# Float16 split of attention probabilities: the high part on ScalarE, with one copy of the row scale

## The chip, the core and the metric

The kernel runs on one core of one Trainium2 chip. The metric is the device time of one execution in microseconds; the kernel before has a median of 892.89 us over 3 runs (891.52 to 894.52).

Five engines share the work, each with its own instruction queue that it works off in order: TensorE (PE; its weight loads are listed as PEld), VectorE (DVE), ScalarE (ACT), GpSimd (POOL), and SyncE (SP), which issues all the DMAs. An engine that meets an instruction whose input is not ready waits, and all that stands behind it waits too.

## The reference

One layer of a streaming encoder on 1024 frames of width 1024. A layer norm, one wide input projection, two attentions side by side (8 heads each), a gated output projection of each, their sum through a last projection, and a post layer norm with residual:

```python
h = layer_norm(x, ln_in_g, ln_in_b)
proj = h @ w_in[l] + b_in[l]
a_q, a_k, a_v, a_z, b_cq, b_ckv, b_kr, b_z, g_a, g_b = jnp.split(proj, pts, axis=-1)
...
s = jnp.einsum('bqhd,bkhd->bhqk', qc, kc) * scale + bias      # mixer A, own chunk and 8 before
p = jax.nn.softmax(s, axis=-1)
ya = jnp.einsum('bhqk,bkhd->bqhd', p, vc)
...
s = jnp.einsum('bqhd,bkhd->bhqk', qb, k) * scale              # mixer B, chunk-causal
p = jax.nn.softmax(s, axis=-1)
yb = jnp.einsum('bhqk,bkhd->bqhd', p, v)
...
mixed = jax.nn.sigmoid(g_a) * ya + jax.nn.sigmoid(g_b) * yb
h = layer_norm(DEEPNORM_ALPHA * h + mixed @ w_out[l], ln_post_g[l], ln_post_b[l])
```

The two softmaxes, and in them the multiplication of the exponentials by the inverse of their row sum, are what the change is about.

## The kernel before, in words

To keep float32 accuracy, every operand of a matmul is split into a high part and a low part. For the dense projections (class `Chunk`, helper `three`, lines 167 to 169) that makes three matmuls: high by high, high by low, low by high. For P.V, the probabilities `p` are scaled by 2^14 and split into two float16 numbers, `hi` = float16(p) and `lo` = float16(p - hi); V is split likewise into the two halves of a 128-column block.

The attention is cut into steps: one head `e` of a head pair `p`, one tile `i` of 128 query rows. Mixer A has 64 steps (stage A, 175 to 390 us) with 128 to 640 key columns each, mixer B 64 steps (stage B, 400 to 740 us) with 128 to 1024. A step is function `softmax` (line 805) and, some steps later, function `pv` (line 822):

- `pair.scores`: TensorE forms the scores in PSUM (lines 692, 693 for A; 789 to 791 for B). VectorE brings them to SBUF with scale and bias and forms the row minimum `nm` (line 697 for A, 796 for B).
- line 808: ScalarE takes the exponential in place, and the row sum `su`.
- line 810: VectorE forms the reciprocal `rc`; line 812: VectorE forms `rc2` = rc * 2^14.
- line 816: GpSimd forms `hi`, with `rc` as a column scale and 2^14 as a constant.
- line 817: VectorE forms `lo` from the exponentials, `rc2` and `hi`.
- line 819: SyncE issues one DMA that transposes `hi` and `lo` into `pT`.
- line 831: TensorE multiplies `pT` with V into `y`; after every fourth step ScalarE (line 721), VectorE (722) and GpSimd (728) finish the head's half.

A step's `pv` is issued 3 steps later in A (`LAG_A`) and 2 steps later in B (`LAG_B`). Between the steps lies dense work for TensorE: projections of coming heads and of the gates, handed out in units by function `run`. Their results leave PSUM through ScalarE and VectorE (lines 642 and 643 for q and k of A, 639 and 640 for B, 710 to 713 for the z gates, 288 for the output gates). Their weights are loaded by SyncE (line 135), copied as high part by ScalarE (131) and subtracted by GpSimd (132). In the last head pair of A and in B the values of B are scaled by GpSimd (531), cast by ScalarE (533) and subtracted by GpSimd (534).

The kernel is written for a tile framework. Python issues the operations in the order above, but the framework's scheduler decides in which order they stand in each engine's queue, from its own estimates. So a change of one operation moves others.

Of the kernel before, what the change touches and what calls it, by code (L numbers as in the profile page):

```python
# [10 lines left out]
F32 = mybir.dt.float32  # L11
F32R = mybir.dt.float32r
I32 = mybir.dt.int32
AF = mybir.ActivationFunctionType
ALU = mybir.AluOpType
# [3 lines left out]
P = 128  # L19
# [36 lines left out]
def tile_hybrid_layer(  # L56
# [25 lines left out]
    V, A, G, SY = nc.vector, nc.scalar, nc.gpsimd, nc.sync  # L82
# [11 lines left out]
    sm = ctx.enter_context(tc.tile_pool(name="sm", bufs=6))  # L94
# [532 lines left out]
    with ExitStack() as p1:  # L627
# [177 lines left out]
        def softmax(pair, e, i, nm_):  # L805
            s, nm, n = pair.scores(e, i)
            su = sm.tile([P, 1], F32, tag="su", name=f"su{nm_}")
            A.activation(s[:, :n], s[:, :n], AF.Exp, scale=-1.0, bias=nm, accum_out=su)  # L808
            rc = sm.tile([P, 1], F32, tag="rc", name=f"rcp{nm_}")
            V.reciprocal(rc, su)  # L810
            rc2 = sm.tile([P, 1], F32, tag="rc2", name=f"rcs{nm_}")
            V.tensor_scalar(rc2, rc, 2.0 ** 14, None, op0=ALU.mult)
            W_ = pools["w"]
            p16 = pools["p"].tile([P, 2 * W_], F16, tag="p16", name=f"p16{nm_}")
            hi, lo = p16[:, :n], p16[:, n : 2 * n]
            G.tensor_scalar(hi, s[:, :n], rc, 2.0 ** 14, op0=ALU.mult, op1=ALU.mult)  # L816
            V.scalar_tensor_tensor(lo, s[:, :n], rc2, hi, op0=ALU.mult, op1=ALU.subtract)  # L817
            pT = pools["pt"].tile([P, 2 * W_ // P, P], F16, tag="pt", name=f"pT{nm_}")
            SY.dma_start(pT[:, : 2 * n // P, :], p16[:, : 2 * n], transpose=True)
            return pT  # L820
# [18 lines left out]
        class Steps:  # L839
# [7 lines left out]
            def one(self):  # L847
                pair, e, i = self.seq[self.at]
                self.at += 1
                nm = f"{self.m}_{2 * pair.p + e}_{i}"  # L850
                self.q.append((pair, e, i, softmax(pair, e, i, nm)))
                if i == 6:
                    self.next_head()
                if len(self.q) > self.lag:
                    self.fin()
# [111 lines left out]
        with ExitStack() as pb:  # L967
# [7 lines left out]
            for p in range(4):  # L975
                u = sb.units(16)
                if p < 3:
                    n = pairsB[p + 1]
# [110 lines left out]
    for j in range(NT):  # L1089
        n = 4 if j == last else 2  # L1090
# [68 lines left out]
```

## Time and profile before

| what | value |
|---|---|
| median of 3 runs | 892.89 us (891.52 to 894.52) |
| the profiled execution | 892.41 us |
| its span, first to last instruction | 890.6 us |
| mean granted clock of TensorE | 0.977 |
| busy: PE, DVE, POOL, ACT | 832.0, 570.3, 397.3, 359.0 us |
| the low part (line 817), stages A and B | 58.2 and 70.2 us |
| the high part (line 816), stages A and B | 45.6 and 49.7 us |

The busy time of an engine is the time in which it has an instruction under way. TensorE's instructions overlap, so its busy share says little of how fast it works; what it waits for, and the granted clock, say more. In a list of waits, "A <- B" reads: A's engine sat idle before A until B was done.

### The profile page before, as it was taken

How to read it: one execution, taken by the hardware profiler on the slowest of the kernel's cores; microseconds unless marked ns; L12 is line 12 of the kernel's file. 1: busy time of each engine (PE TensorE's matmuls, PEld its weight loads, DVE VectorE, ACT ScalarE, POOL GpSimd, SP SyncE). 2: the span in 40 equal slices, each digit the busy share in tenths (PEclk: the TensorE clock that was granted, in tenths of full speed). 3: DMA queues.
4: the chain of work that ended last, by engine and by line, in shares of the span. 5: the costliest groups of instructions: out<-in, count | busy, mean ns of one | idle time of the engine just before them, and what ended most of it. 6: DMA issues, size and time to landing. Idle time of an engine off the chain costs nothing. (4 is left out here: it accounts for less than half of the span.)

```text
span 890.6 us, 13773 instructions
## 1 busy us (share of the span) xinstructions
PE 832.0 (93%) x4760; PEld 697.9 (78%) x4760; DVE 570.3 (64%) x1267; ACT 359.0 (40%) x729; POOL 397.3 (45%) x413
## 2 busy tenths in 40 slices
PE   5999899998999896999999999999998899999996
PEld 4999798887777685778787877888777787888886
DVE  6899655577687769756655655265606584657654
ACT  4234475445455535545443444354425251422000
POOL 5547541344554445834333943253445373641100
PEclk8999899999999999899999999999999899999999
DMA  6522013376678564595665567556866879551421
GB/s 204 204 106 80 32 42 101 139 150 134 147 150 173 128 145 115 99 206 115 141 154 148 107 153 149 163 119 133 186 176 134 197 194 288 178 165 60 142 95 47
DMA packets 185365, 124.68 MB, mean 140 GB/s; under 512 B 146160, under 2 KB 149744, under 8 KB 185296
## 3 DMA queue, kind: packets, MB, share of 16 engines
q1 hardware_dynamic: 185296, 123.82, 56.0%
q8 instruction: 37, 0.61, 0.3%
q14 instruction: 32, 0.26, 0.1%
HBM read 57.98 MB, written 22.81 MB: 91 GB/s over the span
## 5 line engine op out<-in xcount | busy, mean ns | idle before, releaser
L167 PE MATMUL dn<-hT,wh_c 128*128 128x512 f32 x512 | 206.6, 404 | 5.4 <-DVE sK L643 2.3
L169 PE MATMUL dn<-hT,wl_c 128*128 128x512 f32 x512 | 203.8, 398 | 0.0
L168 PE MATMUL dn<-hT,wh_c 128*128 128x512 f32 x512 | 203.3, 397 | 0.0
L132 POOL TENSOR_TENSOR wl_c<-wr_c,wh_c 128x512 fp32r<-128x512 f32 x64 | 86.1, 1346 | 117.7 <-ACT wh_c L131 103.2
L167 PEld LDWEIGHTS dn<-hT,wh_c 128*128 128x128 f32 x512 | 97.8, 191 | 24.6 <-DVE bQ L640 2.4
L169 PEld LDWEIGHTS dn<-hT,wl_c 128*128 128x128 f32 x512 | 97.6, 191 | 20.1
L168 PEld LDWEIGHTS dn<-hT,wh_c 128*128 128x128 f32 x512 | 97.9, 191 | 18.1
L817 DVE SCALAR_TENSOR_TENSOR p<-sbs,rcs,p 128x128 f16<-128x128 f32 (+3 forms) x64 | 70.2, 1099 | 24.7 <-POOL p L816 22.9
L816 POOL TENSOR_SCALAR p<-sbs,rcp 128x128 f16<-128x128 f32 (+3 forms) x64 | 49.7, 777 | 75.0 <-DVE rcp L810 57.8
L131 ACT ACTIVATE wh_c<-wr_c 128x512 fp32r<-128x512 f32 x64 | 40.3, 630 | 84.0 <-DMA wr_c<-in_wch_dram 61.2
L817 DVE SCALAR_TENSOR_TENSOR p<-ss,rcs,p 128x640 f16<-128x640 f32 (+2 forms) x64 | 59.2, 936 | 21.0 <-POOL p L816 19.9
L808 ACT ACTIVATE sbs<-sbs,nmb 128x128 f32<-128x128 f32 (+3 forms) x64 | 49.5, 774 | 56.1 <-DVE sbs L796 49.1
L728 POOL TENSOR_TENSOR yt<-yt,sz 64x512 f32<-64x512 f32 x32 | 43.4, 1355 | 52.5 <-DVE yt L722 35.7
L816 POOL TENSOR_SCALAR p<-ss,rcp 128x640 f16<-128x640 f32 (+2 forms) x64 | 45.6, 717 | 41.5 <-DVE rcp L810 27.9
L808 ACT ACTIVATE ss<-ss,nm 128x640 f32<-128x640 f32 (+2 forms) x64 | 44.4, 694 | 46.4 <-DVE nm L697 39.3
L831 PE MATMUL y<-pT,v16b 128*128 128x128 f16 x576 | 45.4, 222 | 8.6 <-DMA pT<-p 8.4
L169 PE MATMUL ops<-wo,mixT 128*128 128x512 f32 (+1 forms) x144 | 53.1, 369 | 0.0
L168 PE MATMUL ops<-wo,mixT 128*128 128x512 f32 (+1 forms) x144 | 52.9, 369 | 0.0
L831 PEld LDWEIGHTS <-v16b 128*128 128x128 f16 x576 | 33.5, 99 | 23.8 <-issue 22.6
L831 PE MATMUL y<-pT,v16a 128*128 128x128 f16 x480 | 38.4, 223 | 14.6 <-DMA pT<-p 13.4
L167 PE MATMUL ops<-wo,mixT 128*128 128x512 f32 (+1 forms) x144 | 51.7, 369 | 0.0
L831 PEld LDWEIGHTS <-v16a 128*128 128x128 f16 x480 | 28.8, 99 | 26.2 <-issue 21.1
(247 smaller groups left out, 1891.2 us busy)
## 6 DMA issues: line engine op xcount, KB each, us to landing
wr_c<-in_wch_dram SPq DMA_DIRECT2D x64, 256.0 KB, 3.1
th_d<-g SPq DMA_DIRECT2D x32, 256.0 KB, 2.5
th<-th_d SPq DMA_DIRECT2D x32, 256.0 KB, 3.3
h_d<-xt SPq DMA_DIRECT2D x8, 512.0 KB, 2.6
sX<-sQ SPq DMA_DIRECT2D x16, 256.0 KB, 4.6
sXb<-bQ SPq DMA_DIRECT2D x16, 256.0 KB, 3.9
r<-h_d SPq DMA_DIRECT2D x8, 512.0 KB, 3.5
wor<-in_wo_dram SPq DMA_DIRECT2D x16, 256.0 KB, 2.9
```

The costliest lines, as they stand in the source:

```text
L131: A.activation(hi, raw, AF.Copy)
L132: (eng or V).tensor_tensor(lo, raw, f(hi), op=ALU.subtract)
L167: T.matmul(ps, ah, bh, start=start, stop=False)
L168: T.matmul(ps, ah, bl, start=False, stop=False)
L169: T.matmul(ps, al, bh, start=False, stop=stop)
L728: G.tensor_tensor(yt[r, :], yt[r, :], pair.sz[half][r, :], op=ALU.mult)
L808: A.activation(s[:, :n], s[:, :n], AF.Exp, scale=-1.0, bias=nm, accum_out=su)
L816: G.tensor_scalar(hi, s[:, :n], rc, 2.0 ** 14, op0=ALU.mult, op1=ALU.mult)
L817: V.scalar_tensor_tensor(lo, s[:, :n], rc2, hi, op0=ALU.mult, op1=ALU.subtract)
L831: T.matmul(o, v16[:, k0 + k, h % 4, :], pT[:, a * nk + k, :], start=(k == 0 and a == 0), stop=(k == nk - 1 and a == 1))
```

## The change

ScalarE forms `hi`, with a copy activation whose column scale is `rc2`; GpSimd no longer has a part in the softmax. The separate tile `rc` goes: VectorE first multiplies the row sum by 2^-14 and then takes the reciprocal in place, which gives rc * 2^14 as before. Since a line fewer stands in the file, lines behind 810 shift by one: the high part is line 815 now, the low part 816, the transposing DMA 818, P.V 830.

```diff
             A.activation(s[:, :n], s[:, :n], AF.Exp, scale=-1.0, bias=nm, accum_out=su)
-            rc = sm.tile([P, 1], F32, tag="rc", name=f"rcp{nm_}")
-            V.reciprocal(rc, su)
             rc2 = sm.tile([P, 1], F32, tag="rc2", name=f"rcs{nm_}")
-            V.tensor_scalar(rc2, rc, 2.0 ** 14, None, op0=ALU.mult)
+            V.tensor_scalar(rc2, su, 2.0 ** -14, None, op0=ALU.mult)
+            V.reciprocal(rc2, rc2)
             W_ = pools["w"]
             p16 = pools["p"].tile([P, 2 * W_], F16, tag="p16", name=f"p16{nm_}")
             hi, lo = p16[:, :n], p16[:, n : 2 * n]
-            G.tensor_scalar(hi, s[:, :n], rc, 2.0 ** 14, op0=ALU.mult, op1=ALU.mult)
+            A.activation(hi, s[:, :n], AF.Copy, scale=rc2)
             V.scalar_tensor_tensor(lo, s[:, :n], rc2, hi, op0=ALU.mult, op1=ALU.subtract)
```

The scheduler places the 128 high parts among ScalarE's other instructions, and moves others on all engines. First place: ScalarE's queue in the third head of A (head 2), steps 3 to 7. The names: `ss` the exponentials, `su` the row sums, `p` high and low part, `rcs` the row scale, `yl` the half of P.V that ScalarE takes out of PSUM, `zt` and `sz` the z gate, `wh_c` the high part of a weight. Before:

```order
L808 ACTIVATE ss_4_2736,su_2_4_2739<-ss_4_2736,nm_4_2737 128x640
L131 ACTIVATE wh_c_1_2616<-wr_c_1_2615 128x512
L808 ACTIVATE ss_5_2766,su_2_5_2769<-ss_5_2766,nm_5_2767 128x640
L808 ACTIVATE ss_6_2803,su_2_6_2806<-ss_6_2803,nm_6_2804 128x640
L131 ACTIVATE wh_c_0_2851<-wr_c_0_2850 128x512
L721 ACTIVATE yl_2_0_2833<-y_2_0_2717,us_101 64x512
L808 ACTIVATE ss_7_2874,su_2_7_2877<-ss_7_2874,nm_7_2875 128x640
```

and now:

```order
L808 ACTIVATE ss_4_2716,su_2_4_2719<-ss_4_2716,nm_4_2717 128x640
L131 ACTIVATE wh_c_1_2599<-wr_c_1_2598 128x512
L808 ACTIVATE ss_5_2745,su_2_5_2748<-ss_5_2745,nm_5_2746 128x640
L815 ACTIVATE p_2_4_2724<-ss_4_2716,rcs_2_4_2721 128x640
L815 ACTIVATE p_2_5_2753<-ss_5_2745,rcs_2_5_2750 128x640
L131 ACTIVATE wh_c_0_2828<-wr_c_0_2827 128x512
L808 ACTIVATE ss_6_2781,su_2_6_2784<-ss_6_2781,nm_6_2782 128x640
L721 ACTIVATE yl_2_0_2810<-y_2_0_2697,us_101 64x512
L815 ACTIVATE p_2_6_2789<-ss_6_2781,rcs_2_6_2786 128x640
```

The high part of step 4 now stands behind a weight copy and the exponential of step 5, and the exponential of step 6 stands behind two high parts and a weight copy.

Second place: the change from head 6 to head 7 of A (347 to 374 us in the trace). `vs_b` and `v16b` are the values of B, `bK` keys of B. GpSimd's queue before:

```order
L728 TENSOR_TENSOR yt_5_1_4094<-yt_5_1_4094,sz_1_3530 64x512
L531 TENSOR_TENSOR vs_b_0_4099<-v16b_3394,vsc_b_4044 128x256
L816 TENSOR_SCALAR p_6_5_4201<-ss_5_4192,rcp_6_5_4197 128x640
L531 TENSOR_TENSOR vs_b_1_4129<-v16b_3394,vsc_b_4044 128x256
L531 TENSOR_TENSOR vs_b_2_4162<-v16b_3394,vsc_b_4044 128x256
L816 TENSOR_SCALAR p_6_6_4230<-ss_6_4221,rcp_6_6_4226 128x640
L534 TENSOR_TENSOR v16b_3394<-vs_b_0_4099,v16b_3394 128x4x64
L816 TENSOR_SCALAR p_6_7_4296<-ss_7_4287,rcp_6_7_4292 128x640
```

ScalarE's queue there now:

```order
L808 ACTIVATE ss_7_4232,su_6_7_4235<-ss_7_4232,nm_7_4233 128x640
L710 ACTIVATE zt_0_4129<-dn_0_3947,bcolh 128x512
L712 ACTIVATE sz_0_4131<-dn_0_3947,bcol 128x512
L808 ACTIVATE ss_0_4269,su_7_0_4272<-ss_0_4269,nm_0_4270 128x128
L533 ACTIVATE v16b_3358<-vs_b_1_4077 128x4x64
L639 ACTIVATE bK_4113<-bk_0_4115 64x512
L533 ACTIVATE v16b_3358<-vs_b_2_4109 128x4x64
L808 ACTIVATE ss_1_4323,su_7_1_4326<-ss_1_4323,nm_1_4324 128x256
L815 ACTIVATE p_6_7_4240<-ss_7_4232,rcs_6_7_4237 128x640
```

On GpSimd the high parts stood between the scalings of the values of B; on ScalarE the high part of head 6, step 7 stands behind seven other instructions that come after its exponential.

## Rows read from the trace of the kernel before

**Rows 1.** Page, part 1: busy us, share of the span, instructions.

```profile
PE 832.0 (93%) x4760; PEld 697.9 (78%) x4760; DVE 570.3 (64%) x1267; ACT 359.0 (40%) x729; POOL 397.3 (45%) x413
```

**Rows 2.** Windows, stages A, B: length; PE, PEld, DVE, ACT, POOL busy; clock, DMA.

```profile
175.00:390.00 215.00, 195.05 (x1216) 160.25 (x1215) 160.49 (x387) 110.37 (x230) 114.10 (x136) 0.97 0.67 140
400.00:740.00 340.00, 325.70 (x1858) 266.40 (x1857) 193.09 (x460) 145.85 (x285) 156.64 (x149) 0.98 0.67 152
```

**Rows 3.** Waits of PE, stage A, then B: us in total, times, longest.

```profile
PE y L831 <- DMA pT<-p: 13.4, 13, 2.0
PE y L831 <- DMA pT<-p: 8.4, 6, 2.6
```

**Rows 4.** Timeline, DVE and POOL, A's first and last step: start, us.

```profile
174.78 0.16 DVE L810 RECIPROCAL rcp<-su 128x1 f32<-128x1 f32 x1 [0.22 <-ACT ss L808]
174.98 0.15 DVE L812 TENSOR_SCALAR rcs<-rcp 128x1 f32<-128x1 f32 x1
175.12 0.38 POOL L816 TENSOR_SCALAR p<-ss,rcp 128x128 f16<-128x128 f32 x1
...
386.46 0.15 DVE L810 RECIPROCAL rcp<-su 128x1 f32<-128x1 f32 x1
386.97 1.57 POOL L816 TENSOR_SCALAR p<-ss,rcp 128x640 f16<-128x640 f32 x2
```

**Rows 5.** Groups by form: busy us, mean ns of one | idle before.

```profile
L816 POOL TENSOR_SCALAR p<-ss,rcp 128x640 f16<-128x640 f32 x32 | 28.4, 891 | 16.8 <-DVE rcp L810 13.9 <-issue 2.7
L808 ACT ACTIVATE ss<-ss,nm 128x640 f32<-128x640 f32 x32 | 26.5, 827 | 21.3 <-DVE nm L697 19.3 <-DVE rcs L812 1.2 <-DVE rcp L810 0.6
L401 ACT ACTIVATE ct<-ct,rr 128x256 f32<-128x256 f32 x8 | 4.1, 509 | 3.7 <-POOL rr L128 3.5
L808 ACT ACTIVATE ss<-ss,nm 128x256 f32<-128x256 f32 x8 | 4.0, 501 | 1.3 <-POOL p L816 1.3
L817 DVE SCALAR_TENSOR_TENSOR p<-ss,rcs,p 128x640 f16<-128x640 f32 x32 | 36.0, 1138 | 6.6 <-POOL p L816 5.9 <-DVE rcp L810 0.3
L697 DVE CUSTOM_DVE_ANT_0 ss<-sa,tb 128x640 f32<-128x640 f32 x32 | 26.0, 817 | 2.0 <-PE sa L693 1.7
```

**Rows 6.** Page, part 5: the exponentials of stages B and A.

```profile
L808 ACT ACTIVATE sbs<-sbs,nmb 128x128 f32<-128x128 f32 (+3 forms) x64 | 49.5, 774 | 56.1 <-DVE sbs L796 49.1
L808 ACT ACTIVATE ss<-ss,nm 128x640 f32<-128x640 f32 (+2 forms) x64 | 44.4, 694 | 46.4 <-DVE nm L697 39.3
```

**Rows 7.** Windows of line 816 alone, stages A and B: length, POOL busy.

```profile
175.00:390.00 215.00, 45.63 (x64) 0.97 0.67 140
400.00:740.00 340.00, 49.70 (x64) 0.98 0.67 152
```

**Rows 8.** Timeline of ACT, in the second place shown.

```profile
354.97 0.59 ACT L639 ACTIVATE bK<-bk 64x512 fp32r<-64x512 f32 x1
...
356.52 0.69 ACT L710 ACTIVATE zt<-dn,bcolh 128x512 f32<-128x512 f32 x1 [0.21 <-DMA y_d<-yt]
```

**Rows 9.** Waits of ACT and DVE, stage A.

```profile
ACT ss L808 <- DVE nm L697: 35.7, 23, 3.9
ACT wh_c L131 <- DMA wr_c<-in_wch_dram: 16.9, 9, 3.7
DVE p L817 <- POOL p L816: 19.9, 26, 2.6
```

**Rows 10.** Timeline of POOL and DVE near 365 us.

```profile
365.29 0.67 POOL L534 TENSOR_TENSOR v16b<-vs_b,v16b 128x256 f16<-128x256 f32 x1
365.35 1.47 DVE L817 SCALAR_TENSOR_TENSOR p<-ss,rcs,p 128x256 f16<-128x256 f32 x1 [2.64 <-POOL p L816]
```

**Rows 11.** Timeline of PE: two matmuls of 512 columns.

```profile
179.69 0.39 PE L167 MATMUL dn<-hT,wh_c 128*128 128x512 f32 x1
179.92 0.39 PE L168 MATMUL dn<-hT,wh_c 128*128 128x512 f32 x1
```

**Rows 12.** Windows, head 6 to head 7 of A.

```profile
347.00:374.00 27.00, 21.38 (x126) 16.88 (x125) 21.47 (x51) 17.81 (x41) 23.06 (x26) 0.87 0.59 106
```

## The prediction

> **What bounds the kernel now.** I read the page's busy times first. TensorE (PE) is busy 832.0 us, 93% of the span; VectorE (DVE), GpSimd (POOL) and ScalarE (ACT) stand at 64, 45 and 40% [rows 1]. So the question for the change is not how much work it moves but whether TensorE waits more or less. The change touches only the attention, so I cut the trace into its two stages, A (175 to 390 us) and B (400 to 740 us) [rows 2]. There TensorE is idle 215 - 195.05 = 20.0 us and 340 - 325.70 = 14.3 us, and its mean granted clock is 0.97 and 0.98, which costs another 215 x 0.03 + 340 x 0.02 = 13.3 us, or 0.39 us for each us of idle time. VectorE fills 75% of stage A, ScalarE 51%, GpSimd 53%; in B 57, 43 and 46%.
>
> The waits tell which work comes late. TensorE's largest are for the transposed probabilities: 13.4 us in 13 waits in A and 8.4 us in 6 in B [rows 3], 21.8 us together. They are the only stake that the change can reach directly. A softmax step runs: score matmuls, scaling and row minimum (VectorE), exponential with row sum (ScalarE), reciprocal (VectorE), high part (GpSimd), low part (VectorE), transposing DMA, P.V matmuls. TensorE works in program order, so what counts is the margin between the landing of a transposed tile and the moment at which TensorE gets to it.
>
> **The change, part by part.** There are 128 steps, 64 in each stage.
>
> 1. The high part leaves GpSimd. In the timeline I paired each reciprocal with the high part that follows it: the first pair waits 0.18 us, and the last (the second of the two merged high parts, which starts near 387.74) 1.13 us [rows 4]. Over 64 pairs each the mean is 0.78 us in A and 0.47 us in B. That is GpSimd's queue, and it goes.
>
> 2. The operation itself. GpSimd takes 891 ns for 640 columns. ScalarE's price for a float16 output with a column scale from SBUF has no row; the nearest are the exponential at 640 columns, 827 ns, and, for the form, the copy with a column scale at 256 columns, 509 ns beside 501 ns for the exponential [rows 5]. So I price it as the exponential: over all forms it gains 0.03 us a step in A and 0.01 in B. The bounds are -0.1 and +0.1 us.
>
> 3. VectorE's two small operations keep their number. Before, GpSimd needed only the reciprocal; now ScalarE needs both, so one more of 0.15 us with its hand-over stands in the chain [rows 4]: +0.19 us a step.
>
> 4. ScalarE's load. 64 high parts at the exponential's price are 44.4 us in A and 49.5 us in B [rows 6]. ScalarE goes to 154.8 of 215 us (72%) in A and to 195.4 of 340 us (57%) in B. GpSimd falls by its 45.6 and 49.7 us [rows 7].
>
> 5. ScalarE's queue, the disputed term. In the new order, counted over the whole program, 2.1 other ScalarE instructions stand between a step's exponential and its high part in A, 1.2 in B; by the durations of their forms 1.41 and 0.81 us. VectorE needs some 0.95 us (A) and 0.70 us (B) in that time anyway for its two small operations. Only what exceeds this delays the high part: taken step by step, 0.68 us in A and 0.33 us in B. The second place shown is an extreme: seven instructions between, about 4.0 us by their forms, among them a gate evacuation at 0.69 and a key half at 0.59 us [rows 8].
>
> 6. Waits inside that queue. ScalarE too works in order, and those instructions wait themselves: in A exponentials wait 35.7 us for VectorE's minimum, 0.56 us each over 64, and weight copies 16.9 us for their load, 0.77 us each over 22 [rows 9]. An exponential stands between in 30 of 64 steps, a weight copy in 18: 0.56 x 30/64 + 0.77 x 18/64 = 0.48 us a step at most. None of it counts where VectorE's small operations are late for the same reason. Between 0 and 0.48 I take 0.25 us, in both stages.
>
> 7. The low part on VectorE. It takes 1138 ns at 640 columns, where the 640-column operation with only one SBUF tensor takes 817 [rows 5]; it stretches when GpSimd works beside it, as at 365.35 us (1.47 us for 256 columns, beside a GpSimd subtraction) [rows 10]. Of 46 low parts that were slowed by more than 0.1 us, 35 overlapped a two-input GpSimd operation, which stays. So the relief is between 0 and 0.25 us a step; I take 0.05, and leave it out of the sum. The Trainium skill ("GPSIMD Engine Reference", Specifications) says that GpSimd's SBUF interface is shared with VectorE and contends with VectorE instructions that have two SBUF inputs. The trace agrees as far as the stretched low parts go; by that rule alone the relief would be the larger one, which is a rival below.
>
> 8. Cover on TensorE. The scheduler has reordered its matmuls too. Pricing each 512-column matmul by the 0.23 us from start to start [rows 11] and the other forms likewise, 10.75 us of matmuls stood between a step's last score matmul and its first P.V matmul in A, and 11.17 us stand there now: +0.42 us. In B it is 13.32 and 13.23: -0.08.
>
> **The sum.** Chain in A: 0.19 + 0.68 + 0.25 - 0.78 - 0.03 = +0.31 us against +0.42 of cover; in B 0.19 + 0.33 + 0.25 - 0.47 - 0.01 = +0.29 against -0.08. On the mean that is nearly level, but waits are one-sided: a step that gains where nobody waited gives nothing. So I took each of the 128 steps' margins in the trace (minus the wait where TensorE waited), added its own change of cover and subtracted its own change of chain. The negative margins sum to 27.4 us before and 33.7 us after: +6.3. The rows put down 21.8 of those 27.4 us as waits, so I take 0.8 of it, 5.0 us. More idle time lowers the clock; 0.39 of it would be 2.0 us, and I take half, since the grant falls only in some stretches: the costliest, 347 to 374 us, has 0.87 and GpSimd busy 23.06 of 27 us [rows 12]. Together +6.0 us. The profiled execution took 892.41 us, 0.48 below the median of the three runs: 898.4 us.
>
> **The rivals.**
>
> *GpSimd's backlog was the trouble: faster.* At 347 to 374 us GpSimd is the fullest engine beside TensorE, and the high parts stand in one queue with its casts and subtractions. If ScalarE is free whenever VectorE delivers the scale, terms 5 and 6 vanish, and the same count over the steps gives 18.5 us: -8.9 x 0.8 = -7.1, with half the clock's share -1.4, so 883.9 us. It decides at a mean queue wait on ScalarE of about 0.68 us in A: below that the kernel gains. For it speak ScalarE's short operations, 0.4 to 0.8 us; against it the new order, which puts the high part behind others in 60 of 64 steps of A.
>
> *Level.* If the waits inside the queue never count, the count is 27.2 us: 892.3 us. For it speaks the added cover.
>
> *The port.* If removing the high parts takes the whole stretch off the low parts (0.22 us a step in A, 0.28 in B, 32 us of VectorE's time), that cancels term 6: again near 892.3 us. Against it stand the 35 of 46. The skill's rule named above would have it so.
>
> *Head of the line.* If the whole 0.48 us counts, the count is about 42.4 us: +15.0 x 0.8 = 12.0, and 2.3 of clock: 906.7 us. For it speaks that a weight load stands on the DMA queue behind transposes that wait for the low part, so that a late high part makes the next weight copy late.
>
> *The change doesn't do what it says.* The order excludes it: all 128 rows left GpSimd and stand on ScalarE, and no further table load appears.
>
> **How the numbers follow.** About 0.3%, 2.7 us, is what a measurement of this kernel can tell from no change. My forecast, 898.4 us, has 0.33, the head of the line 0.12: slower 0.45. Level has 0.17 and the port 0.08: same 0.25. The backlog has 0.30: faster. The range must hold most of the backlog case and of the head of the line: 881 to 912 us. The likeliest case's own range is 895 to 904.
>
> **What would show it.** The exponential-priced high part: 0.75 to 0.90 us at 640 columns on ScalarE. ScalarE busy near 155 us in A. TensorE's waits for transposed tiles: above 25 us if I am right, below 16 if the backlog was the trouble. The low part at 640 columns: above 1.05 us if GpSimd's two-input operations stretch it, near 0.88 if the port rival holds. VectorE's waits for the high part (19.9 us in A before [rows 9]) should grow. I am wrong if TensorE waits less although ScalarE's queue holds the high part longer than 0.7 us: then the cover, not the chain, decides.

## The result and the profile after

The changed kernel took **881.55 us** (median of 4 runs, 880.07 to 882.12) where the kernel before, on the same chip, took 892.83 us (4 runs, 891.52 to 894.52): a ratio of **0.987, with a 95% interval of 0.9849 to 0.9891**. I had forecast 898.4 us. The sign was wrong; the time lies at the low end of the range (881 to 912 us). A second measurement beside other kernels gave 882.18 us and 0.9867 [0.9837, 0.9897].

First the busy times of the page, the line that answers to [rows 1], and then the windows of stages A and B, which answer to [rows 2] (length; PE, PEld, DVE, ACT, POOL busy; clock, DMA):

```profile
PE 827.7 (94%) x4760; PEld 693.2 (79%) x4760; DVE 554.0 (63%) x1267; ACT 441.9 (50%) x857; POOL 299.6 (34%) x285
```

```profile
175.00:390.00 215.00, 198.04 (x1249) 161.82 (x1248) 156.07 (x392) 149.35 (x296) 69.55 (x77) 0.98 0.73 145
400.00:740.00 340.00, 332.02 (x1906) 271.91 (x1905) 180.60 (x456) 188.66 (x341) 108.64 (x87) 0.99 0.70 161
```

The move itself stands there much as forecast: ScalarE took on 83 us (forecast 93.9), GpSimd lost 98 us (forecast 95.3). What was not forecast is in the DVE column. VectorE has the same 1267 instructions, and yet 16.3 us less work over the span (570.3 to 554.0), 4.4 us less in the window of A and 12.5 in that of B. The page's groups of instructions show where. Of the kernel before, the low parts of stages B and A, and then of the changed kernel (busy us, mean ns of one | idle before):

```profile
L817 DVE SCALAR_TENSOR_TENSOR p<-sbs,rcs,p 128x128 f16<-128x128 f32 (+3 forms) x64 | 70.2, 1099 | 24.7 <-POOL p L816 22.9
L817 DVE SCALAR_TENSOR_TENSOR p<-ss,rcs,p 128x640 f16<-128x640 f32 (+2 forms) x64 | 59.2, 936 | 21.0 <-POOL p L816 19.9
```

```profile
L816 DVE SCALAR_TENSOR_TENSOR p<-sbs,rcs,p 128x128 f16<-128x128 f32 (+3 forms) x64 | 57.1, 898 | 28.3 <-ACT p L815 27.8
L816 DVE SCALAR_TENSOR_TENSOR p<-ss,rcs,p 128x640 f16<-128x640 f32 (+2 forms) x64 | 54.6, 867 | 19.8 <-ACT p L815 18.9
```

The same 128 low parts cost 129.4 us before and 111.7 us now: 13.1 us less in B, 4.6 us in A. All of VectorE's saving is this one line.

The waits of TensorE in stages A and B, to hold against [rows 3]:

```profile
PE y L830 <- DMA pT<-p: 10.2, 16, 1.7
PE y L830 <- DMA pT<-p: 3.9, 5, 1.7
```

They fell from 21.8 to 14.1 us. The high part on ScalarE, its exponential and the low part at 640 columns in stage A, by form, to hold against [rows 5]:

```profile
L808 ACT ACTIVATE ss<-ss,nm 128x640 f32<-128x640 f32 x32 | 26.4, 826 | 13.9 <-DVE nm L697 9.0 <-DVE rcs L810 2.5 <-DVE rcs L811 2.1
L815 ACT ACTIVATE p<-ss,rcs 128x640 f16<-128x640 f32 x32 | 25.8, 821 | 2.8 <-ACT ss L808 1.4 <-DMA pT<-p 1.4
...
L816 DVE SCALAR_TENSOR_TENSOR p<-ss,rcs,p 128x640 f16<-128x640 f32 x32 | 32.9, 1036 | 10.9 <-ACT p L815 10.4
```

And the waits of ScalarE and VectorE in stage A, to hold against [rows 9]:

```profile
ACT ss L808 <- DVE nm L697: 22.6, 22, 3.7
ACT wh_c L131 <- DMA wr_c<-in_wch_dram: 13.7, 8, 3.2
```

```profile
DVE p L816 <- ACT p L815: 18.9, 21, 3.8
```

I took the chain of every step apart (start of the exponential to landing of the transposed tile; means over 64 steps). In **stage A it got longer**, 8.20 to 8.66 us: the wait in the queue of the engine that forms the high part rose from 0.78 us (GpSimd) to 1.04 us (ScalarE), and the time from the low part's end to the landing, which no term of the prediction has, from 3.85 to 4.06 us. In **stage B it got shorter**, 8.06 to 7.77 us: that wait stayed (0.47 to 0.46), the low part fell from 1.10 to 0.90 us, and the gap ahead of it from 0.37 to 0.21. So in A TensorE waits less behind a longer chain, which the prediction had named as the sign that it was wrong.

Why the low part got shorter is seen in one step of stage B. Timeline of GpSimd and VectorE in the kernel before (start, us):

```profile
446.37 0.80 POOL L816 TENSOR_SCALAR p<-sbs,rcp 128x640 f16<-128x640 f32 x1 [1.84 <-DVE rcs L812]
447.13 1.29 POOL L132 TENSOR_TENSOR wl_c<-wr_c,wh_c 128x512 fp32r<-128x512 f32 x1
447.20 1.91 DVE L817 SCALAR_TENSOR_TENSOR p<-sbs,rcs,p 128x640 f16<-128x640 f32 x1 [0.18 <-POOL p L816]
```

and of the same step in the changed kernel:

```profile
441.05 1.29 POOL L132 TENSOR_TENSOR wl_c<-wr_c,wh_c 128x512 fp32r<-128x512 f32 x1 [4.77 <-ACT wh_c L131]
...
442.36 0.83 ACT L815 ACTIVATE p<-sbs,rcs 128x640 f16<-128x640 f32 x1 [0.62 <-DVE rcs L811]
...
443.21 0.69 ACT L288 ACTIVATE g<-dn,bcolh 128x512 f32<-128x512 f32 x1
443.22 0.88 DVE L816 SCALAR_TENSOR_TENSOR p<-sbs,rcs,p 128x640 f16<-128x640 f32 x1 [0.95 <-ACT p L815]
```

Before, the end of the high part released two things at the same moment: VectorE's low part, and GpSimd's own queue, whose next entry, a weight subtraction, had waited behind it. The two ran side by side, and the low part took 1.91 us, where the same step's low part takes 0.88 in the changed kernel. Now a weight subtraction stands 2 us ahead of the low part, beside other work of VectorE; what starts together with the low part is a ScalarE operation, and nothing stretches. Against the shortest durations in the kernel before at each width (0.35 us at 128 columns to 1.28 at 1024), 42 of the 128 low parts were longer by over 0.3 us before, 19 are now: 20 to 15 in A, but 22 to 4 in B. Every one of them overlapped a GpSimd instruction. And 54 low parts started within 0.2 us of a GpSimd instruction's start before, 16 do now.

### The profile page after: what moved, and what is told of

Its sections match the earlier page's. It is cut to its first block, busy times and chain, and to the rows that moved or that the text cites. A ratio compares the mean times of both kernels' runs of the same rounds, so it can differ in the third digit from the quotient of the medians.

```text
span 879.3 us, 13755 instructions
## 1 busy us (share of the span) xinstructions
PE 827.7 (94%) x4760; PEld 693.2 (79%) x4760; DVE 554.0 (63%) x1267; ACT 441.9 (50%) x857; POOL 299.6 (34%) x285
## 5 line engine op out<-in xcount | busy, mean ns | idle before, releaser
L167 PE MATMUL dn<-hT,wh_c 128*128 128x512 f32 x512 | 204.7, 400 | 2.1 <-DVE bQ L640 1.0
L169 PE MATMUL dn<-hT,wl_c 128*128 128x512 f32 x512 | 201.3, 393 | 0.0
L168 PE MATMUL dn<-hT,wh_c 128*128 128x512 f32 x512 | 200.8, 392 | 0.0
L132 POOL TENSOR_TENSOR wl_c<-wr_c,wh_c 128x512 fp32r<-128x512 f32 x64 | 83.9, 1310 | 226.8 <-ACT wh_c L131 214.5
L167 PEld LDWEIGHTS dn<-hT,wh_c 128*128 128x128 f32 x512 | 96.7, 189 | 20.2 <-DVE bQ L640 1.4
L168 PEld LDWEIGHTS dn<-hT,wh_c 128*128 128x128 f32 x512 | 96.7, 189 | 17.5
L816 DVE SCALAR_TENSOR_TENSOR p<-sbs,rcs,p 128x128 f16<-128x128 f32 (+3 forms) x64 | 57.1, 898 | 28.3 <-ACT p L815 27.8
L816 DVE SCALAR_TENSOR_TENSOR p<-ss,rcs,p 128x640 f16<-128x640 f32 (+2 forms) x64 | 54.6, 867 | 19.8 <-ACT p L815 18.9
L810 DVE TENSOR_SCALAR rcs<-su 128x1 f32<-128x1 f32 x128 | 19.3, 152 | 62.4 <-ACT sbs L808 45.2
L815 ACT ACTIVATE p<-sbs,rcs 128x128 f16<-128x128 f32 (+3 forms) x64 | 48.8, 771 | 13.0 <-ACT sbs L808 7.2
L796 DVE TENSOR_SCALAR_CACHE_REDUCE sbs<-sb 128x128 f32<-128x128 f32 (+3 forms) x64 | 47.9, 755 | 1.5
L830 PE MATMUL y<-pT,v16a 128*128 128x128 f16 x480 | 39.0, 223 | 10.2 <-DMA pT<-p 10.2
```

Source lines behind the costliest of these rows:

```text
L132: (eng or V).tensor_tensor(lo, raw, f(hi), op=ALU.subtract)
L167: T.matmul(ps, ah, bh, start=start, stop=False)
L168: T.matmul(ps, ah, bl, start=False, stop=False)
L169: T.matmul(ps, al, bh, start=False, stop=stop)
L796: V.tensor_scalar(s[:, :n].rearrange("p (b w) -> p b w", b=nb), ps[:, :nb, :w], -B_SCALE, None, op0=ALU.mult, op1=ALU.min, accum_out=nm,)
L810: V.tensor_scalar(rc2, su, 2.0 ** -14, None, op0=ALU.mult)
```

## The experiments

Two theories stood at the start. **Place**: what counts is that GpSimd stands no longer between the row scale and the low part. **Load**: what counts is that GpSimd does less, through VectorE's stretched operations. A third soon came in, the **order**: the scheduler had also laid out TensorE's matmuls anew. To part these I held TensorE's matmuls to a given order with ordering edges that add no semaphore wait; the scheduler still ordered the other engines. Ratios are against runs of the kernel before on the same chip.

**1. TensorE's order alone, and the engine alone.** The changed kernel with TensorE's matmuls in the order of the kernel before, and the kernel before with those of the changed one:

```
+ at = [k for a, n in TENSOR_ORDER for k in range(a, a + n)]
+ for a, b in zip(at, at[1:]):
+     tc.add_manual_dep(mm[b], mm[a].name, info, reason="tensor order")
```

> The change as it is (high part on ScalarE), but with TensorE's 4760 matmuls held to the order in which they stood before the change. Order theory (the scheduler's new TensorE order gives the late probabilities more cover): the gain goes, 889 to 893 us. Port theory (the low part on VectorE is no longer stretched by GpSimd) and backlog theory (GpSimd's queue held the high part up): the gain stays, 880 to 885 us.

Measured: 886.25 us, 0.9926 [0.9901, 0.9951].

> The kernel before (high part on GpSimd), but with TensorE's matmuls held to the order that the change got. Order theory: 881 to 886 us. Port and backlog theories: no gain, 890 to 895 us.

Measured: 897.05 us, 1.0043 [1.0024, 1.0061]. The change pays in the old order; the new order under GpSimd's chain is a loss. The order theory fell in its simple form: the order is no gift of its own. But the change in the old order gives only 0.74% of the 1.3%, so the rest needs the order that was laid out for it.

**2. The change in one stage only.** In each kernel the other stage keeps the old lines:

```
+ if isinstance(pair, PairA):
+     V.tensor_scalar(rc2, su, 2.0 ** -14, None, op0=ALU.mult)
+     V.reciprocal(rc2, rc2)
+ else:
+     rc = sm.tile([P, 1], F32, tag="rc", name=f"rcp{nm_}")
+     V.reciprocal(rc, su)
+     V.tensor_scalar(rc2, rc, 2.0 ** 14, None, op0=ALU.mult)
...
+ if isinstance(pair, PairA):
+     A.activation(hi, s[:, :n], AF.Copy, scale=rc2)
+ else:
+     G.tensor_scalar(hi, s[:, :n], rc, 2.0 ** 14, op0=ALU.mult, op1=ALU.mult)
```

The second kernel has `PairB` in place of `PairA`.

> The change in the 64 steps of mixer A alone; mixer B keeps GpSimd. Port theory: of the 17 us by which the low parts got shorter 13 lie in B, so A alone brings little, 888 to 892 us. Order theory: A has the added cover (+0.42 us a step against -0.08 in B), so A alone brings most of it, 881 to 886 us. Backlog theory: most in A as well, since GpSimd's queue held the high part up for 0.78 us there and for 0.47 us in B.

Measured: 887.42 us, 0.9942 [0.9917, 0.9966].

> The change in the 64 steps of mixer B alone; mixer A keeps GpSimd. Port theory: most of the gain, 882 to 886 us. Order and backlog theories: little, 888 to 893 us.

Measured: 891.49 us, 0.9977 [0.9954, 0.9999]. Both stages gain, and A, where the chain became longer, not less than B. The two intervals together reach the 1.3%, their middles give 0.8%, so whether the stages add up is not settled by this. It speaks against a reckoning by the low parts alone: 13 of the 17 us by which they got shorter lie in B, for which B alone was expected at 882 to 886 us.

**3. GpSimd's load put back, first in a form that misled.** An unused copy on GpSimd beside each ScalarE high part:

```
+ junk = pools["j"].tile([P, W_], F16, tag="junk", name=f"jk{nm_}")
+ G.tensor_scalar(junk[:, :n], s[:, :n], rc2, None, op0=ALU.mult)
  A.activation(hi, s[:, :n], AF.Copy, scale=rc2)
```

> The changed kernel, with TensorE's matmuls held in its own order, and beside each ScalarE high part a copy of the same operation on GpSimd (same input, same scale, same width, result never used). GpSimd's work is that of the kernel before again (about 94 us more in the two stages), but nothing waits for it. Load theory (what was gained is GpSimd's shorter queue and its lighter use of SBUF, wherever its result goes): most of the gain is lost, 888 to 893 us, low parts about 60 us in A and 70 us in B as before. Chain theory (the gain is that GpSimd no longer stands between the scale and the low part, so that its next operation does not start together with the low part): 880 to 885 us, low parts within 4 us of the changed kernel's 55.5 and 57.5 us.

Measured: 898.82 us, 1.0039 [1.002, 1.0059]. This did not put back the same load. By form, GpSimd's group in this kernel:

```profile
L816 POOL TENSOR_SCALAR jk<-ss,rcs 128x640 f16<-128x640 f32 x32 | 63.4, 1982 | 11.7 <-DVE rcs L811 5.8 <-ACT ss L808 4.4
```

The operation with one scalar takes 1982 ns for 640 columns where the one with two scalars of the kernel before takes 891 [rows 5]. The load was over twice that meant, so the run tells only that a heavily loaded GpSimd costs more than the change had gained.

The form with two scalars (scale and 1.0) mends it:

> As the kernel with the unused GpSimd copy beside each ScalarE high part, but the copy in the form with two scalars (scale and 1.0) that the kernel before used, since the one-scalar form took 1982 ns for 640 columns where the two-scalar form took 891 ns. GpSimd's load is now within 3 us a stage of that of the kernel before. Load theory: 887 to 893 us, as before the change. Chain theory (only GpSimd's place between scale and low part counted): 880 to 885 us.

Measured: 889.16 us, 0.9951 [0.9924, 0.9979], with 925 ns at 640 columns and GpSimd busy 400.8 us (397.3 before). An operation whose result nobody reads gave back, by the ratios, 0.8 of the 1.3%. The low parts in its groups, stages B and A:

```profile
L818 DVE SCALAR_TENSOR_TENSOR p<-sbs,rcs,p 128x128 f16<-128x128 f32 (+3 forms) x64 | 65.6, 1034 | 28.4 <-ACT p L817 28.1
L818 DVE SCALAR_TENSOR_TENSOR p<-ss,rcs,p 128x640 f16<-128x640 f32 (+2 forms) x64 | 60.1, 952 | 20.3 <-ACT p L817 19.4
```

125.7 us against 111.7: of the 17.7 us of relief, 14.0 are gone again. By my expectation the load theory has this one. The copy also reads the exponentials and could hold their buffer; but in the waits that ended with it, other engines lost 0.3 us in this kernel and 0.8 us in that of experiment 4, so that is not where the time went.

**4. The same in the old order**, so that GpSimd's load and TensorE's order are as in the kernel before; the place of the useful high part and the row scale in one copy are new:

> The high part on ScalarE, an unused GpSimd copy of the same width beside it (two-scalar form), and TensorE's matmuls held in the order of the kernel before. Against the kernel before only the place of the useful high part differs; GpSimd's load and TensorE's order are the same. If GpSimd's load (through VectorE's stretched operations) is what the change pays off: 891 to 896 us, low parts about 130 us in sum, as before. If taking GpSimd out of the chain is what counts: 884 to 888 us, as with the old order and no copy (886.3).

Measured: 895.65 us, 1.0015 [0.9992, 1.0039]. The low parts, stages A and B:

```profile
L818 DVE SCALAR_TENSOR_TENSOR p<-ss,rcs,p 128x640 f16<-128x640 f32 (+2 forms) x64 | 65.9, 1043 | 21.9 <-ACT p L817 21.5
L818 DVE SCALAR_TENSOR_TENSOR p<-sbs,rcs,p 128x128 f16<-128x128 f32 (+3 forms) x64 | 63.8, 1005 | 25.0 <-ACT p L817 23.0 <-DMA qr<-qr_d 1.3 <-DMA pT<-p 0.4
```

With order and load kept, the two parts of the change together are worth nothing that can be measured; experiment 6 takes them apart. The ratios make a table:

| high part on | GpSimd's load | TensorE order before | TensorE order of the changed kernel |
|---|---|---|---|
| GpSimd | as before | 1 | 1.0043 |
| ScalarE | as before (unused copy) | 1.0015 | 0.9951 |
| ScalarE | without the high parts | 0.9926 | 0.987 |

Read down the last two rows: **the load is worth 0.9% in the old order and 0.8% in the new**. Read along them: the new order is worth 0.6% with either load, but only with the high part on ScalarE. That is the account of the 1.3%. The changed kernel was not run with its own order held; two kernels held in that order that differ from it by small operations on VectorE alone (experiments 7 and 9) came to 0.9845 and 0.9885, on either side of its 0.987, so holding an order shows no cost of its own.

**5. An operation that starts with the low part.** The unused operation now waits for the high part, so that it starts when the low part does: once with two SBUF inputs and at most 256 columns, once with one input and full width.

```
  A.activation(hi, s[:, :n], AF.Copy, scale=rc2)
+ G.tensor_tensor(junk[:, :w_], s[:, :w_], hi[:, :w_], op=ALU.subtract)     # first kernel
+ G.tensor_scalar(junk[:, :n], hi, 2.0, 1.0, op0=ALU.mult, op1=ALU.mult)    # second kernel
```

> The changed kernel, TensorE's matmuls in its own order, with one GpSimd subtraction of at most 256 columns (two SBUF inputs, result never used) that becomes ready at the moment at which the low part does. This puts back the suspected cost, a GpSimd operation that starts together with the low part. Overlap theory: the low parts stretch again by 0.15 to 0.4 us each, their sum goes from 113 us to 125 to 145 us, and the time to 886 to 893 us. If the low part's length does not matter for the end, or does not stretch: 880 to 884 us.

Measured: 893.2 us, 0.9983 [0.9962, 1.0005]; over 0.3 us too long were 48 low parts.

> The changed kernel, TensorE's matmuls in its own order, with an unused one-input GpSimd copy (two immediate scalars, full width, about 0.9 us at 640 columns) that becomes ready when the high part is done, so that it starts together with the low part. If any GpSimd operation stretches the low part, the low parts' sum goes from 113 us to 125 us or more and the time to 889 to 895 us. If only GpSimd operations with two SBUF inputs stretch it, the sum stays below 118 us and the time within 2 us of the kernel whose unused copy runs beside the high part.

Measured: 893.3 us, 0.9979 [0.9958, 1.0]; 38 such low parts, their sum up by 13 us. Both gave back nearly the whole gain, the first with operations of 256 columns at most. Neither kind of GpSimd operation leaves the low part alone, so the two-input ones, on which the prediction rested, are not the only ones that stretch it. GpSimd was busy 418.5 and 419.5 us in these two, some 18 us longer than with the copy of experiment 3, so the moment of the start is not the only difference between them.

**6. The second part of the change alone.** The row scale in one copy, the high part still on GpSimd, TensorE in the old order:

```
- rc = sm.tile([P, 1], F32, tag="rc", name=f"rcp{nm_}")
- V.reciprocal(rc, su)
- V.tensor_scalar(rc2, rc, 2.0 ** 14, None, op0=ALU.mult)
+ V.tensor_scalar(rc2, su, 2.0 ** -14, None, op0=ALU.mult)
+ V.reciprocal(rc2, rc2)
- G.tensor_scalar(hi, s[:, :n], rc, 2.0 ** 14, op0=ALU.mult, op1=ALU.mult)
+ G.tensor_scalar(hi, s[:, :n], rc2, None, op0=ALU.mult)                      # first kernel
+ G.tensor_scalar(hi, s[:, :n], rc2, 1.0, op0=ALU.mult, op1=ALU.mult)         # second kernel
```

> The kernel before with only the second part of the change: the high part stays on GpSimd, but takes the one combined scale, so that both small VectorE operations stand ahead of it; TensorE's matmuls are held in the order of the kernel before. By term 3 the chain gets 0.19 us longer in each of 128 steps: 893.5 to 897 us. Rival, that a one-scalar operation on GpSimd is shorter than its two-scalar one or that VectorE needs the second operation in that time anyway: 890 to 893.5 us.

Measured: 925.97 us, 1.0345 [1.0314, 1.0376]; here too the one-scalar form, 1934 ns at 640 columns, spoils the run.

> The row scale in one copy with the high part still on GpSimd, now in the two-scalar form (combined scale and 1.0); TensorE's order is that of the kernel before. High parts of 0.89 us at 640 columns on GpSimd. By term 3, one more small VectorE operation of 0.19 us in the chain of each step: 893.5 to 897 us. Rival, that this operation hides beside GpSimd's queue wait (0.78 us a step in A): 891 to 893.5 us.

Measured: 906.39 us, 1.0147 [1.0128, 1.0166], far beyond what I had expected of one small operation. The waits of TensorE, stage A and stage B:

```profile
PE y L830 <- DMA pT<-p: 25.8, 21, 5.8
PE y L830 <- DMA pT<-p: 15.1, 11, 4.8
```

They are nearly twice those of [rows 3]. The chain grew by 0.71 us in A and 0.33 in B, since a later scale also met a longer GpSimd queue (1.07 us in place of 0.78). So in the old order, with the high part on GpSimd, a longer chain goes straight to the end. And the place counts after all: the kernel of experiment 4 (1.0015) has the same row scale, the same order and an unused operation where this one has its high part on GpSimd. Between the two, taking the useful high part out of GpSimd's queue is worth 1.3%. In the change, that gain was used up by the row scale in one copy.

**7. One small operation less.** In the changed kernel the reciprocal alone is left between row sum and high part; the factor 2^14 is left out of the probabilities, and the scale of the output makes up for it (2^-16 in place of 2^-30):

```
- V.tensor_scalar(rc2, su, 2.0 ** -14, None, op0=ALU.mult)
- V.reciprocal(rc2, rc2)
+ V.reciprocal(rc2, su)
```

> The changed kernel without the second small VectorE operation: the probabilities are kept without the factor 2^14 and the output scale is 2^-16 in place of 2^-30, so that the reciprocal alone stands between the row sum and the high part. TensorE's matmuls are held in the changed kernel's order. The chain falls by about 0.3 us a step. If the chain still sets TensorE's waits as steeply as in the kernel with the scale alone (67 us of chain cost 13 us): 873 to 877 us. If the order of the changed kernel has cover enough and only a few steps wait: 878 to 882 us.

Measured: 881.7 us, 0.9845 [0.9818, 0.9872].

> The same without the second small operation, with TensorE's order left to the scheduler (it comes out with 10.9 us of cover in A and 13.18 in B, against 11.17 and 13.23). Chain theory: within 3 us of the held one, 872 to 880 us. If the order decides more than the chain: 880 to 888 us.

Measured: 887.73 us, 0.9918 [0.989, 0.9946]. Held, the kernel is level with the changed one (882.18 us beside it). With the order left free it loses 6 us. The small operation did stand in the chain: without it, held, the high part of A starts 1.57 us after its exponential in place of 1.93, and A's chain falls from 8.66 to 8.27 us. Yet TensorE waited 14.6 us for transposed tiles, where it had waited 14.1. In this order a shorter mean chain was worth nothing.

**8. One more step of lag in stage A.** `LAG_A = 4` in place of 3.

> The changed kernel with one more step between softmax and P.V in stage A (LAG_A 4 in place of 3, one more buffer for transposed tiles). If the chain of a softmax step still bounds stage A, its 10.2 us of waits for transposed tiles fall below 4 us and the time to 870 to 877 us. If TensorE's order and the other engines bound it, the waits turn up at the score matmuls or at the dense work: 878 to 884 us.

Measured: 887.28 us, 0.9903 [0.9884, 0.9923]. A's waits for transposed tiles stayed (10.7 us); the scheduler used the larger lag for an order whose cover is 11.8 us in place of 11.17. Both of my expectations missed it. It is no way to a better kernel, and a sign that orders differ by a third of a per cent (0.9903 against 0.987) for reasons that a mean cover does not show.

**9. Is it VectorE's time?** If the stretch costs time because VectorE is busy, VectorE time without GpSimd must cost the same. One or three unused operations on one column, between high and low part:

```
  A.activation(hi, s[:, :n], AF.Copy, scale=rc2)
+ V.tensor_scalar(sm.tile([P, 1], F32, tag="jk", name=f"jk0{nm_}"), hi[:, 0:1], 1.0, None, op0=ALU.mult)
```

> The changed kernel, TensorE's matmuls in its own order, with one unused VectorE operation on one column between the high part and the low part of each step. 128 such operations cost VectorE about 14 us (the kernel without the second small operation had 14.0 us less VectorE time), which is what the unused GpSimd copies took from the low parts (14.2 us). If VectorE's lost time is how GpSimd's load reaches the end: 886 to 891 us. If GpSimd's load works in another way (its own queue, the DMA queue behind it): 880 to 884 us.

Measured: 883.42 us, 0.9908 [0.9884, 0.9932]. By my expectation this speaks against VectorE's lost time as the way in which GpSimd's load reaches the end. But VectorE was busy only 9.5 us longer than in the changed kernel (563.5 us), not 14, and a loss of 0.4% for 9.5 us does not differ, within the intervals, from 0.8% for the 14.0 us of experiment 3. The run decides nothing.

> The same with three unused VectorE operations in each step, about 42 us of VectorE time and 0.33 us or more in each chain. If VectorE's time counts: 895 to 910 us. If not even this counts: under 886 us.

Measured: 894.91 us, 1.0047 [1.0029, 1.0065]. Then the same three behind the low part (they read `lo`, after the transposing DMA is issued):

> As the kernel with three unused VectorE operations in each step, but they stand behind the low part and read it, so they are in no step's own chain and only take VectorE's time (about 25 us more than in the changed kernel). If VectorE's time as such is what reaches the end: 890 to 896 us, near the 894.9 of the three operations ahead of the low part. If only what stands in a softmax step's chain counts: 881 to 885 us.

Measured: 880.88 us, 0.9885 [0.9847, 0.9923]. The busy times of the two kernels with three operations, ahead of the low part and behind it:

```profile
PE 833.7 (93%) x4760; PEld 697.8 (78%) x4760; DVE 578.8 (64%) x1651; ACT 440.9 (49%) x857; POOL 302.0 (34%) x285
```

```profile
PE 826.6 (94%) x4760; PEld 693.1 (79%) x4760; DVE 576.3 (65%) x1651; ACT 441.5 (50%) x857; POOL 303.6 (34%) x285
```

578.8 and 576.3 us of VectorE work, 1.6% apart in time. VectorE's sum as such is free here: 576 us is more than the kernel before had. What cost time was what stood ahead of a step's own low part, and GpSimd's next operation struck the low part itself.

**10. The scatter.**

> The changed kernel once more, beside these three on the same chip: 880 to 884 us. Its second profile tells how far the sums of one stage scatter between executions; where they scatter by 3 us or more, no difference of that size between two kernels' stages is read as an effect.

Measured: 882.18 us, 0.9867 [0.9837, 0.9897]. Between the two profiles of the changed kernel TensorE's idle time in A and B, summed matmul by matmul, differs by 0.9 and 1.9 us. I read no stage difference below 3 us as an effect.

## Why the prediction was wrong, step by step

- **Term 7, the low part, is the step that failed first.** I gave 0 to 0.25 us a step, took 0.05 and left it out of the sum. It measured 4.6 us over 64 steps in A (0.07 a step) and 13.1 us in B (0.20 a step). The reason I gave, "35 overlapped a two-input GpSimd operation, which stays", counted overlaps and not what made them: the operations stayed, but the high part no longer released them at the moment at which it released the low part. Of the 46 slowed low parts 29 overlapped a weight subtraction, of the 23 that are slowed as much now 11 do; and 17 of the 46 overlapped the high part of another step, which left. Term 4 gave no price at all to the work that leaves GpSimd; the runs with the unused copy show that it is worth 0.8 to 0.9%, 7 to 8 us of the 11. The Trainium skill's rule that I had set against it ("GPSIMD Engine Reference", Specifications: GpSimd and VectorE share an SBUF interface, and VectorE instructions with two SBUF inputs contend for it) had the right sign. The traces agree: the low parts lost 17.7 us with GpSimd's high parts, and 14.0 us came back with the unused copy.
- **The margin count failed too, in stage A.** With term 7 whole, as in the port rival, it still gave 892.3 us. I put each step's measured change of chain into it, in place of the terms. In B it then gives 3.0 us of negative margins, where 3.9 was measured (8.4 before): there the sizes were wrong and the count was right. In A it gives 21.8 us, where 10.2 was measured (14.5 before): there it would have been wrong with every size right. The longer waits that it adds up did not come; why, no run shows.
- **Terms 5 and 6, ScalarE's queue, were right in A and too large in B.** From the exponential's end to the high part's start I had forecast +0.34 us in A (0.19 + 0.68 + 0.25 - 0.78) and +0.30 in B; measured were +0.35 and +0.13. The whole chain of A grew by 0.46 where I had 0.31, since the landing came 0.20 us later. In B it was +0.29 forecast and -0.29 measured: the low part makes 0.20 of the difference, the gap ahead of it 0.17 and the earlier start of the high part 0.17.
- **Terms 1, 2 and 4 were right in what they priced.** The high part takes 821 ns at 640 columns, beside 827 forecast; ScalarE is busy 149.35 us in A, where I had 154.8.
- **Term 3, the second small operation, was too large.** Of its 0.19 us the scale came 0.08 us later in A and 0.14 in B. Taking the operation out shortened the chain and changed no time (881.7 against 882.18). On GpSimd in the old order the same operation costs 1.5%, some 13 us.
- **Term 8, cover, had the right sign and the wrong measure.** The mean cover rose by 0.42 us in A, as much as the chain did. Yet the new order is worth 0.6%, and it costs 0.43% under the chain for which it was not made. Neither the mean nor the count step by step holds that.
- **The rivals.** The backlog rival gave the nearest time, 883.9 us, by a mechanism that did not happen: its own condition was a queue wait below 0.68 us, and 1.04 was measured. The sign that I had set for it, waits for transposed tiles below 16 us, came nevertheless (14.1 us). The port rival named the operation that changed, but priced it at no more than term 6 and came to 892.3 us. Its sign, a low part of 0.88 us at 640 columns, came in B (0.89) and not in A (1.04). VectorE's waits for the high part, which should have grown, fell from 19.9 to 18.9 us in A. The sentence "I am wrong if TensorE waits less although ScalarE's queue holds the high part longer than 0.7 us" came true; its second half, that the cover then decides, is half of the account at most.

What is shown and what is not: that GpSimd's load costs 0.8 to 0.9%, with nothing waiting for its result, is shown in two orders. That it does so through the low part is argued. For it speak that the stretch came and went with the load (42 long low parts before, 19 after, 37 and 45 with the unused copy), that VectorE's time outside the step's chain is free, and that in no list of waits does TensorE wait for GpSimd directly. The head of the step, which VectorE works too, also came later with the copy: from the start of the last score matmul to the landing it took 11.83 us in place of 11.41 in B, and 12.16 in place of 12.05 in A. Against it speak experiment 2, where B alone has most of the relief and gained least, and experiment 7, where a shorter chain gained nothing. From the exponential on, mean chains hardly moved when the load came back (8.66 to 8.71 us in A, 7.77 to 7.94 in B), and TensorE's lost time was spread over many waits of 1 to 2 us, for transposed tiles (14.1 to 16.6 us), row minima and keys. A kernel with the load and without the overlap was not tried. So the way from GpSimd's load to the end stays open.

## What to carry to other kernels

When an operation leaves a queue, ask not only how long the queue was but what its end released at the same moment: two engines released together keep running side by side, step after step, and a stretched operation in the chain may be the price. Count overlaps by their cause before you call them permanent. Where a change has two parts, run each alone: here the row scale cost 1.5% and the move gave 1.3%, and neither shows in their sum. And where a scheduler lays out the order anew, take the order apart from the edit: hold one and change the other, since half a per cent either way lies in the order alone.

## What the chip showed unexpectedly

- GpSimd's multiplication with **one** scalar took 1934 to 1982 ns for 640 columns (f32 to f16) in stage A, where the same with **two** took 883 to 925 ns. A second scalar of 1.0 halves the time.
- A 640-column low part on VectorE took 1.91 us beside a GpSimd subtraction of 1.29 us, and 0.88 us without: in this step the overlap cost more than the operation itself.
- One unused GpSimd operation per step, off every chain, cost 0.8%; some 22 us of unused VectorE operations behind the low part cost nothing that could be measured.
